# Two-layer hybrid backbone on one core: packed early loads, own tiles for the mLSTM's z gates, the second layer's output gate by a broadcast DMA

## The chip, the cores and the metric

The kernel runs on one core of a Trainium2 chip. The metric is device time in microseconds (us) of one execution; lower is better. Before the change the median of three runs is 1688.14 us (1687.44 to 1690.84).

## What is computed

Two layers act on 256 latent tokens `x` and 256 context tokens `ctx` of width 1024. The modulation of a layer comes from `c` (for the latent tokens) and `c_ctx` (for the context). One input projection feeds three branches (a bidirectional state-space scan, differential attention, a bidirectional mLSTM), whose outputs are gated, projected, merged and projected once more. Cut to what matters here:

```python
shift, scale, gate = split(silu(c) @ w_mod + b_mod, 3)           # 1024 -> 3 * 1024, per layer
h = rms_norm(x, norm_g) * (1 + scale) + shift
p = [h @ w for w in split_cols(w_in, IN_SIZES)]                  # 14 parts
y_a = ssd_branch(p[0], p[1], p[2], ...)                          # x/B/C with a conv, z, dt
y_b = diff_branch(p[3], p[4], p[5], p[6], ...)                   # q, k, v, z
y_c = mlstm_branch(p[7], ..., p[12], ...)                        # qk, v, o, z, input and forget gates
g = sigmoid(p[13])
x = x + gate * ((g0 * (y_a @ w_branch[0]) + g1 * (y_b @ w_branch[1]) + g2 * (y_c @ w_branch[2])) @ w_out)
# the same for the context with c_ctx; only the latent stream of the last layer is returned
```

## The kernel before

All numbers are fp32. A product is made of three matmuls on parts that are rounded to fp32r: a weight is split into `whi` (ACT casts, L117) and `wlo` (DVE subtracts, L83), an activation into `hh` and `hl`, and the three matmuls are whi by hh, whi by hl and wlo by hh (L146 to L148 with tokens as rows, L177 to L179 in `proj_ch` with channels as rows). Weights arrive in granules of 512 KB (128x4x256, tile `raw`, three buffers), loaded by SP (L128).

The order of the work is not written out. A scheduler sorts each engine's instructions at build time by a priority (band 0: loads and evictions, band 1: the branches' chains, band 2: projection matmuls as filling) and by its own clock; the number of buffers of a tile limits how far a piece can run ahead. SP's loads leave in this order, from one queue.

The places that the change and the prediction's steps touch:

- **Start.** `mod_pair` (L243) loads 4 granules of `w_mod` for each of two column blocks (L255), multiplies each by the vectors in `mod_mm` (L226) and ends in `mod_tail` (L235), which adds `b_mod` into `modc`. It runs twice for layer 0, 16 granules in all: pair one serves the columns k 0 to 3, pair two k 4 to 7. Tile `wm` has 8 buffers; the last three granules go to `raw` buffers. Between the granules SP issues small loads from a list `few` (L352 to L375), two per granule in pair one and three in pair two. The four x loads (L390) come after four granules. `columns(l)` (L395) transposes a layer's rows of small parameters with 12 matmuls.
- **Normalisation of layer 0** (L468 to L511): `turn` transposes the scaled rows (L493, two per k and half), ACT applies the modulation (`hf`), POOL makes `hh` (L89) and DVE `hl` (L83).
- **Narrow gate weights** (L540 to L555): six loads of 16 or 4 columns into one `raw` tile that DVE clears first (L541, L544), the split, then the matmuls of `pg`.
- **Tables**: `narrow` (L287) has the small per-layer columns `gcol`, the products `gcs`/`gsn` of the rotary table and the norm gains, and lambda.
- **Scan of the mLSTM**, `ml_core` (L1086): per direction and chunk the matmuls L1112 (`pw` by `va`), L1117 (`uq` by the state `C`) and L1133 (`kw` by `va`), with DVE between them: `nu`, `dn` (four steps), `y`, `kw`, `C`. Its gates `zz` have two buffers, shared with the other branches' (`silu2`, L719).
- **Output gate**, L1280 to L1294: a vector per token group is spread over 128 partitions by 8 matmuls with the identity (two groups of four, L1292) and halved by ACT (L1294); DVE uses `gbc` at the very end.

Of the kernel before, what the change touches and what calls it, by code (L numbers as in the profile page):

```python
# [18 lines left out]
D = 1024  # L19
# [10 lines left out]
NR = 64  # L30
ACC, PE_, PM = 3, 3, 2
# [3 lines left out]
def hybrid_backbone_kernel(ctx: ExitStack, tc: tile.TileContext, A, out, dbg=None):  # L35
# [128 lines left out]
    def proj_ch(srcs, lhs, ranges, evac, halves=False, gr=None):  # L164
# [3 lines left out]
        with band(2):  # L168
            for i in range(2):
                ps.append(pacc())  # L170
# [25 lines left out]
        for i in range(2):  # L196
            with band(0):
                evac(i, ps[i])

# [31 lines left out]
    def mod_tail(l, cbs, row):  # L231
        with band(2):
# [3 lines left out]
            for x, cb in enumerate(cbs):  # L236
                r = 16 * l + 12 + cb // 3
# [5 lines left out]
    def mod_pair(l, cbs, pool, bufs, rbufs, between=None, each=None, end=False):  # L243
        with band(2):
            ps = pacc()
            for x, cb in enumerate(cbs):
                if x and between:
                    between()
                for k0 in range(0, KT, 2):
                    if end and x and k0 >= 2:  # L250
                        wm = mk(wts, [P, 2, 512], "raw", bufs=3)
                    else:
                        wm = mk(pool, [P, 2, 512], "wm", bufs=bufs)
# [6 lines left out]
                    mod_mm(ps, x, k0, wm)  # L260
# [26 lines left out]
    def narrow(l, pool):  # L287
# [3 lines left out]
        lamt = mk(pool, [P, 4, 64], "lamt", bufs=1)  # L291
        lp = mk(pool, [P, 2, 64], "lp", bufs=1)
# [47 lines left out]
    prow = [mk(setup, [16, 1536], f"prow{l}") for l in range(depth)]  # L340
    with band(0):
# [5 lines left out]
        for l in range(depth):  # L347
            V.memset(prow[l], 0.0)
# [3 lines left out]
        few = []  # L352
        for l in range(depth):
            w_ = prow[l]

            few += [
                (w_[12:14, :], A["b_mod"][l].rearrange("(a n) -> a n", a=2)),
                (w_[8:9, 0:D], A["norm_g"][l : l + 1]),
                (w_[0:3, :], A["ssd_conv_w"][l]),
                (w_[3:4, :], A["ssd_conv_b"][l : l + 1]),  # L360
                (w_[4:7, 0:D], A["ml_conv_w"][l]),
                (w_[7:8, 0:D], A["ml_conv_b"][l : l + 1]),
                (w_[9:10, 0:D], A["ssd_norm_g"][l : l + 1]),
                (w_[10:11, 0:D], A["ml_norm_g"][l : l + 1]),
                (w_[11:12, 0:P], A["diff_subln_g"][l : l + 1]),
            ]
            if l == 0:
                few += [(selm, A["k_selm"]), (sgn, A["k_sgn"])]
                nar = narrow(0, setup)
                few += nar[0]  # L370
                few += [(rope, A["k_rope"].rearrange("a t p d -> p a t d"))]
# [4 lines left out]

# [15 lines left out]
    def columns(l):  # L392
        pc = pm()
        for k in range(12):
            T.transpose(pc[:, 16 * k : 16 * k + 16], prow[l][:, k * P : (k + 1) * P], ident[0:16, 0:16])  # L395
        pl_ = pcols[:, :, 16 * l : 16 * l + 16]
        V.tensor_copy(pl_, pc[:, 0:192].rearrange("p (k a) -> p k a", a=16))

        tsc(pl_[:, :, 0:8], pl_[:, :, 0:8], 0.5, ALU.mult)
        lam_init = 0.8 - 0.6 * math.exp(-0.3 * l)  # L400
        tsc(pl_[:, 0, 11:12], pl_[:, 0, 11:12], 0.5 * (1.0 - lam_init), ALU.mult)
# [6 lines left out]
    first_gr = granules(bc_cols(0, 0))  # L408
    first_gr = chain([next(first_gr)], first_gr)
    mods += [  # L410
        mod_pair(0, (1, 3), setup, 8, 2, None, lambda: few_loads(3), end=True),
    ]
    with band(0):
        few_loads(99)
        columns(0)
    for t in mods:
        t()
    with band(0):
        nar[1]()
# [22 lines left out]
    for l in range(depth):  # L442
# [9 lines left out]
        pr = 16 * l  # L452
        pcol = lambda k, r: pcols[:, k, pr + r : pr + r + 1]
        wcol = lambda c, n=256: w_in[:, c : c + n]
        lam_init = 0.8 - 0.6 * math.exp(-0.3 * l)

        gcol, dbc, nlam, gcs, gsn, gctx = nar[2]
# [5 lines left out]
        with band(1):  # L463
# [19 lines left out]
            def gains(kh):  # L483
                ks = slice(4 * kh, 4 * kh + 4)
                tsc(ga[:, ks, :], modc[l][:, 8 + 4 * kh : 12 + 4 * kh, :], 1.0, ALU.add)
                tt(ga[:, ks, :], ga[:, ks, :], bc(pcols[:, ks, pr + 8], 2), ALU.mult)
# [12 lines left out]
            if l == 0:  # L499
                norm(0)  # L500
                norm(1)
                for kh in range(2):
                    gains(kh)
                    for s in range(2):
                        turn(kh, s)
            else:
                for kh in range(2):
                    gains(kh)
                for s in range(2):
                    norm(s)  # L510
                    for kh in range(2):  # L511
                        turn(kh, s)
# [4 lines left out]
        if l == 0:  # L517
            with band(0):
                for l_ in range(1, depth):
                    columns(l_)  # L520
            setup.release()
# [17 lines left out]
        with band(0):  # L539
            wsm = mk(wts, [P, KT, P], "raw", bufs=3)  # L540
            V.memset(wsm, 0.0)  # L541
            pieces = ((0, O_DT, 16), (16, O_FG, 4), (32, O_DT + 16, 16), (48, O_FG + 4, 4), (80, O_IG, 4), (112, O_IG + 4, 4))
            for c, o, n in pieces:
                nc.sync.dma_start(wsm[:, :, c : c + n], w_in[:, o : o + n].rearrange("(k p) n -> p k n", p=P))  # L544
            wsh = mk(wts, [P, KT, P], "whi", F32R, bufs=3)
            wsl = mk(wts, [P, KT, P], "wlo", F32R, bufs=3)
            split(wsm, wsh, wsl)
        with band(2):
# [866 lines left out]
```

## Time and profile before

| | |
|---|---|
| median of 3 runs | 1688.14 us (1687.44 to 1690.84) |
| profiled execution | 1688.44 us, span 1686.7 us |
| mean granted TensorE clock | 0.992 |
| PE busy | 1649.9 us, 98% of the span |
| weight loads (PEld) busy | 1470.5 us, 87% |
| DVE busy | 1093.0 us, 65% |
| ACT busy | 765.4 us, 45% |
| POOL busy | 185.1 us, 11% |
| HBM | 193.29 MB read, 116 GB/s over the span |

The span is the stretch of the profile from the first to the last instruction; 1.7 us of the execution lie around it. The page cuts the span into 40 slices of 42.2 us and shows the busy share of each in tenths, and PEclk, the granted clock, in the same way. A window is a stretch that the reader chooses; it has the busy time of each engine, the granted clock, the busy share of the 16 DMA engines and their rate. In a timeline each row is one instruction or a run of equal ones, with the idle time of its engine before it and what ended that. Matmuls overlap, so the pitch of their starts, not the duration shown, is what each adds.

### The profile page before, as it was taken

The page shows a single profiled execution, that of the slowest core. Times are in us where ns is not written, and L with a number is a line of the kernel's source. Part 1 is how long each engine was busy: PE and PEld are TensorE (multiplying, and loading weights), DVE is VectorE, ACT ScalarE, POOL GpSimd, SP SyncE. Part 2 cuts the span into 40 slices and gives each one's busy share as a digit, 9 for nine tenths or more (in the row PEclk, how much of TensorE's full clock was granted, in tenths as well). Part 3 has the DMA queues.
Part 4 walks back from the last instruction along what each step waited for, and adds up shares of the span by engine and source line. Part 5 has one row for each costly group of instructions (what it writes and reads, how often), then busy time and mean ns, then how long its engine had stood idle before and what let it go on. Part 6 is the DMA issues. An engine that isn't in the chain of part 4 may idle for free. (4 is left out here: it accounts for less than half of the span.)

```text
span 1686.7 us, 28784 instructions
## 1 busy us (share of the span) xinstructions
PE 1649.9 (98%) x11288; PEld 1470.5 (87%) x11288; DVE 1093.0 (65%) x2175; ACT 765.4 (45%) x1497; POOL 185.1 (11%) x232
## 2 busy tenths in 40 slices
PE   6999999999999999999999999999999999999998
PEld 2798789999899999977777789988899999999998
DVE  4787887767864776523334355796887767775565
ACT  3467534554554543422223233556455555444453
POOL 0114331001100000000010001022122011000100
PEclk8999999999999999999999999999999999999999
DMA  8445322222223222453544442344342325336654
GB/s 273 119 134 160 88 79 79 69 71 63 78 63 101 79 85 64 128 187 93 182 136 128 161 135 59 93 127 135 107 116 76 100 76 141 110 101 176 183 168 150
DMA packets 203653, 197.00 MB, mean 117 GB/s; under 512 B 21855, under 2 KB 184033, under 8 KB 203517
## 3 DMA queue, kind: packets, MB, share of 16 engines
q1 hardware_dynamic: 203516, 195.16, 39.4%
q8 instruction: 89, 1.46, 0.3%
q14 instruction: 48, 0.39, 0.1%
HBM read 193.29 MB, written 1.84 MB: 116 GB/s over the span
## 5 line engine op out<-in xcount | busy, mean ns | idle before, releaser
L83 DVE TENSOR_TENSOR wlo<-raw,whi 128x1024 fp32r<-128x1024 f32 x274 | 347.1, 1267 | 313.8 <-ACT whi L117 312.4
L147 PE MATMUL acc<-wlo,hh 128*128 128x256 f32 x1728 | 504.4, 292 | 0.0
L146 PE MATMUL acc<-whi,hh 128*128 128x256 f32 x1728 | 502.3, 291 | 0.0
L148 PE MATMUL acc<-whi,hl 128*128 128x256 f32 x1728 | 501.5, 290 | 0.0
L117 ACT CAST whi<-raw 128x1024 fp32r<-128x1024 f32 x274 | 287.1, 1048 | 378.1 <-PE acc L178 253.0
L147 PEld LDWEIGHTS acc<-wlo,hh 128*128 128x128 f32 x1728 | 330.1, 191 | 12.5 <-issue 9.5
L148 PEld LDWEIGHTS acc<-whi,hl 128*128 128x128 f32 x1728 | 330.2, 191 | 12.2 <-issue 10.6
L146 PEld LDWEIGHTS acc<-whi,hh 128*128 128x128 f32 x1728 | 329.8, 191 | 11.0 <-issue 8.5
L177 PE MATMUL acc<-hh,whi 128*128 128x512 f32 (+1 forms) x712 | 254.1, 359 | 1.3 <-DVE cv_a L80 1.3
L178 PE MATMUL acc<-hl,whi 128*128 128x512 f32 (+1 forms) x712 | 253.7, 357 | 0.2 <-DVE hl L83 0.2
L179 PE MATMUL acc<-hh,wlo 128*128 128x512 f32 (+1 forms) x712 | 253.1, 357 | 0.0
L177 PEld LDWEIGHTS acc<-hh,whi 128*128 128x128 f32 x712 | 135.0, 191 | 28.3 <-issue 5.9
L178 PEld LDWEIGHTS acc<-hl,whi 128*128 128x128 f32 x712 | 135.4, 190 | 19.4 <-issue 2.4
L179 PEld LDWEIGHTS acc<-hh,wlo 128*128 128x128 f32 x712 | 135.3, 190 | 19.3 <-issue 1.8
L177 PE MATMUL acc<-yh,whi 128*128 128x512 f32 (+1 forms) x384 | 128.7, 338 | 0.0
L178 PE MATMUL acc<-yl,whi 128*128 128x512 f32 (+1 forms) x384 | 128.2, 336 | 0.0
L179 PE MATMUL acc<-yh,wlo 128*128 128x512 f32 (+1 forms) x384 | 128.1, 336 | 0.0
L179 PEld LDWEIGHTS acc<-yh,wlo 128*128 128x128 f32 x384 | 71.9, 188 | 8.3
L178 PEld LDWEIGHTS acc<-yl,whi 128*128 128x128 f32 x384 | 72.1, 188 | 8.0
L968 ACT ACTIVATE E<-pe,nmax 128x512 f32<-128x512 f32 (+1 forms) x96 | 58.7, 616 | 44.8 <-DVE nmax L966 44.6
L177 PEld LDWEIGHTS acc<-yh,whi 128*128 128x128 f32 x384 | 72.0, 188 | 7.3
L811 ACT ACTIVATE ex<-ex,col 128x128 f32<-128x128 f32 x192 | 60.4, 393 | 34.8 <-POOL ex L766 31.0
(302 smaller groups left out, 2429.3 us busy)
## 6 DMA issues: line engine op xcount, KB each, us to landing
raw<-in_w_in_dram SPq DMA_DIRECT2D x192, 512.0 KB
raw<-in_w_branch_dram SPq DMA_DIRECT2D x48, 512.0 KB
wm<-in_w_mod_dram SPq DMA_DIRECT2D x45, 512.0 KB
raw<-in_w_in_dram SPq DMA_DIRECT2D x48, 256.0 KB
ex<-acs_d SPq DMA_DIRECT2D x32, 256.0 KB
raw<-in_w_out_dram SPq DMA_DIRECT2D x16, 512.0 KB
ex<-acs_d SPq DMA_DIRECT2D x32, 128.0 KB
pw<-nm_d SPq DMA_DIRECT2D x8, 256.0 KB
```

The lines of the kernel that those rows point to most:

```text
L83: (eng or V).tensor_tensor(out=o, in0=a, in1=b, op=op)
L117: S.copy(hi, raw)
L146: T.matmul(o, lhsT=xh[:, k, sl], rhs=hi[:, j, :], start=(k == 0 and i == 0), stop=False)
L147: T.matmul(o, lhsT=xh[:, k, sl], rhs=lo[:, j, :], start=False, stop=False)
L148: T.matmul(o, lhsT=xl[:, k, sl], rhs=hi[:, j, :], start=False, stop=(k == KT - 1 and i == 1))
L177: T.matmul(o, lhsT=hi[:, j, cs], rhs=xh[:, k, a:b], start=(k == 0 and first), stop=False)
L178: T.matmul(o, lhsT=hi[:, j, cs], rhs=xl[:, k, a:b], start=False, stop=False)
L179: T.matmul(o, lhsT=lo[:, j, cs], rhs=xh[:, k, a:b], start=False, stop=(k == KT - 1 and final))
L811: S.activation(ex[:, c, :], ex[:, c, :], AF.Exp, bias=col[:, LDT, c, d, h : h + 1])
L968: S.activation(e_, o, AF.Exp, bias=ng[:, m : m + 1], accum_out=rs[:, m : m + 1])
```

## The change

1. **Small loads.** The rows of both layers come packed in two tiles, one DMA per parameter: `mrow_` (b_mod, norm_g) and `prow` (the rest). One small load stands behind each `w_mod` granule instead of two or three; both tiles are transposed before the projections. The loads of `narrow` and the rotary table move behind the `w_mod` loads. `wm` has 11 buffers. The matmuls of the modulation are issued for two granules at once.
2. **First projections.** The first granule of the x projection is loaded early too, and the first two projections (B/C and x) alternate by granule, the x one in the `pe` PSUM banks; `turn` goes k by k.
3. **Narrow gate weights.** Two loads (32 and 16 columns) into a tile of their own and three DVE copies (L545 of the changed kernel) instead of six loads.
4. **z gates of the mLSTM** get own tiles (`mzz`, four buffers).
5. **Output gate of the last layer.** The vector is written to DRAM (`gate_d`) and read back over 128 partitions by one DMA; DVE halves it. The 8 matmuls and 2 ACT instructions of that layer go.

The core of the diff:

```diff
-    def proj_ch(srcs, lhs, ranges, evac, halves=False, gr=None):
+    def proj_ch(srcs, lhs, ranges, evac, halves=False, gr=None, bank=None):
...
-                ps.append(pacc())
+                ps.append((bank or pacc)())
...
+                yield
...
-                    if end and x and k0 >= 2:
-                        wm = mk(wts, [P, 2, 512], "raw", bufs=3)
-                    else:
-                        wm = mk(pool, [P, 2, 512], "wm", bufs=bufs)
+                held = []
+                    wm = mk(pool, [P, 2, 512], "wm", bufs=bufs)
...
-                    mod_mm(ps, x, k0, wm)
+                    held.append((k0, wm))
+                    if len(held) == 2:
+
+                        for k_, w_ in held:
+                            mod_mm(ps, x, k_, w_)
+                        held = []
...
+        few = [
+            (mrow_[0:4, :], A["b_mod"].rearrange("l (a n) -> (l a) n", a=2)),
+            (mrow_[4:6, 0:D], A["norm_g"]),
+            (selm, A["k_selm"]),
+            (prow[0:6, :], A["ssd_conv_w"].rearrange("l k n -> (l k) n")),
...
+            (sgn, A["k_sgn"]),
+        ]
...
-    mods = [mod_pair(0, (0, 2), setup, 8, 2, load_x, lambda: few_loads(2))]
+    mods = [mod_pair(0, (0, 2), setup, 11, 2, load_x, lambda: few_loads(1))]
+
+    first_gr = [granules(bc_cols(0, 0)), granules([A["w_in"][0][:, O_X : O_X + 256]])]
+    first_gr = [chain([next(g)], g) for g in first_gr]
...
-                for k in range(4 * kh, 4 * kh + 4):
-                    pt = (pe if k % 2 else pm)()[:, 0:256]
+                for k in kh:
+                    pt = (pe if k % 2 and l else pm)()[:, 0:256]
...
-                    for s in range(2):
-                        turn(kh, s)
+                    for k in range(4 * kh, 4 * kh + 4):
+                        for s in range(2):
+                            turn((k,), s)
...
+            wnr = mk(wts, [P, KT, 48], "raw", bufs=3)
-            pieces = ((0, O_DT, 16), (16, O_FG, 4), (32, O_DT + 16, 16), (48, O_FG + 4, 4), (80, O_IG, 4), (112, O_IG + 4, 4))
-            for c, o, n in pieces:
-                nc.sync.dma_start(wsm[:, :, c : c + n], w_in[:, o : o + n].rearrange("(k p) n -> p k n", p=P))
+            for c, o, n in ((0, O_DT, 32), (32, O_IG, 16)):
+                nc.sync.dma_start(wnr[:, :, c : c + n], w_in[:, o : o + n].rearrange("(k p) n -> p k n", p=P))
...
+                V.tensor_copy(v4(wsm[:, :, h_ : h_ + 64])[:, :, :, c % 64 : c % 64 + n], v4(wnr[:, :, o : o + 2 * n]))
+            if l == 0:
...
+                for p_ in nar[0][4:] + nar[0][:4]:
+                    nc.sync.dma_start(*p_)
+                nc.sync.dma_start(rope, A["k_rope"].rearrange("a t p d -> p a t d"))
...
-            zz = mk(ev, [P, 2, 256], "zz", bufs=2)
+            zz = mk(own, [P, 2, 256], "mzz", bufs=4) if own else mk(ev, [P, 2, 256], "zz", bufs=2)
...
-        bc_proj(0)
-        x_proj(0, 0)
-        x_proj(0, 1)
+        if l == 0:
+            run(zip_longest(bc_proj(0), x_proj(0, 0)))
+        else:
+            run(bc_proj(0))
+            run(x_proj(0, 0))
+        run(x_proj(0, 1))
...
+        if last:
+            gate_d = mk(rows_d, [D], "gate_d")
+            with band(2):
+                nc.sync.dma_start(gate_d.rearrange("(k p) -> p k", p=P), modc[l][:, 16:24, 0])
...
+                if last:
+
+                    with band(0):
+                        nc.sync.dma_start(gbc[p], gate_d.partition_broadcast(P))
+                    tsc(gbc[p], gbc[p], 0.5, ALU.mult)
+                    continue
```

What this does to the order, at three places.

SP at the start, before: the first `w_mod` loads with the small loads of `few` between them.

```order
L255 DMA wm<-in_w_mod_dram 128x2x512
L375 DMA prow_98<-in_b_mod_dram 2x1536
L375 DMA prow_98<-in_norm_g_dram 1x1024
L255 DMA wm<-in_w_mod_dram 128x2x512
L375 DMA prow_98<-in_ssd_conv_w_dram 3x1536
L375 DMA prow_98<-in_ssd_conv_b_dram 1x1536
L255 DMA wm<-in_w_mod_dram 128x2x512
```

SP at the same place in the changed kernel.

```order
L260 DMA wm<-in_w_mod_dram 128x2x512
L378 DMA mrow__98<-in_b_mod_dram 4x1536
L260 DMA wm<-in_w_mod_dram 128x2x512
L378 DMA mrow__98<-in_norm_g_dram 2x1024
L260 DMA wm<-in_w_mod_dram 128x2x512
L378 DMA selm<-in_k_selm_dram 128x4
```

One small load stands between two granules instead of two; ahead of the last `w_mod` load SP issues 57 loads before and 38 in the changed kernel, among these one more granule of 512 KB.

DVE at the start, before: the last rotary products, the `hl` of pair one (eight), the clearing of the narrow weights' tile, then the modulation and the `hl` of pair two.

```order
L83 TENSOR_TENSOR gcs<-rope,gctx 128x64
L83 TENSOR_TENSOR gsn<-rope,gctx 128x64
L83 TENSOR_TENSOR hl<-hf,hh 128x256 x8
L541 MEMSET raw 128x1024
L83 TENSOR_TENSOR modc<-acc,pcols 128x8 x2
L87 TENSOR_SCALAR ga<-modc 128x8
L83 TENSOR_TENSOR ga<-ga,pcols 128x8
L83 TENSOR_TENSOR wlo<-raw,whi 128x1024
L83 TENSOR_TENSOR hl<-hf,hh 128x256 x4
```

DVE in the changed kernel: two `hl` for k 0, then these rows (`hl` two at a time; L545 are the copies of the narrow weights; the L85 row on `raw` is lambda's).

```order
L85 TENSOR_TENSOR gcs<-rope,gctx 128x64
L85 TENSOR_TENSOR gsn<-rope,gctx 128x64
L545 COPY raw<-raw 128x8x2x16
L545 COPY raw<-raw 128x8x2x4 x2
L85 TENSOR_TENSOR hl<-hf,hh 128x256
L530 MEMSET sv 64x12
L85 TENSOR_TENSOR modc<-acc,pcols 128x8 x2
L85 TENSOR_TENSOR raw<-raw 128x128
L85 TENSOR_TENSOR hl<-hf,hh 128x256
L89 TENSOR_SCALAR ga<-modc 128x8
```

The `hl` for k 2 and 3 now stand behind the rotary products and the copies of the narrow weights, and so behind the two loads that these wait for.

PE in the first head of layer 0's mLSTM scan (`ml_core(0)`), before, with the numbers that tell the tiles apart.

```order
L177 MATMUL acc_6458<-hh_294,whi_6462 128x512
L178 MATMUL acc_6458<-hl_295,whi_6462 128x512
L1112 MATMUL pm_6312<-va_5164,pw_6286 128x257
L1117 MATMUL pe_6316<-C_6310,uq_5154 128x257
L1133 MATMUL pm_6327<-va_5164,kw_6325 128x257
L179 MATMUL acc_6458<-hh_294,wlo_6463 128x512
L177 MATMUL acc_6458<-hh_294,whi_6493 128x512
L178 MATMUL acc_6458<-hl_295,whi_6493 128x512
```

PE in the same scan in the changed kernel, where L1112, L1117 and L1133 are L1128, L1133 and L1149.

```order
L149 MATMUL acc_6808<-wlo_6867,hh_266 128x256
L150 MATMUL acc_6808<-whi_6866,hl_267 128x256
L1128 MATMUL pm_6320<-va_5153,pw_6275 128x257
L1133 MATMUL pe_6324<-C_6318,uq_5143 128x257
L1149 MATMUL pm_6335<-va_5153,kw_6333 128x257
L1128 MATMUL pm_6339<-va_5153,pw_6275 128x257
L1133 MATMUL pe_6343<-C_6337,uq_5143 128x257
L1128 MATMUL pm_6362<-va_5153,pw_6352 128x257
L1149 MATMUL pm_6374<-va_5153,kw_6372 128x257
L1128 MATMUL pm_6378<-va_5153,pw_6352 128x257
L1133 MATMUL pe_6382<-C_6376,uq_5143 128x257
L1149 MATMUL pm_6393<-va_5153,kw_6391 128x257
```

Before, 9 to 22 projection matmuls stand between two steps of this scan; in the changed kernel 17 matmuls of the scan follow each other with two projection matmuls among them, and then the four transposes of the next head.

## Rows read from the trace of the kernel before

**Rows 1.** The page: busy time of the engines, and PE's busy tenths in 40 slices.

```profile
PE 1649.9 (98%) x11288; PEld 1470.5 (87%) x11288; DVE 1093.0 (65%) x2175; ACT 765.4 (45%) x1497; POOL 185.1 (11%) x232
...
PE   6999999999999999999999999999999999999998
```

**Rows 2.** Windows at the start: us, busy times, PEclk, DMA share, GB/s.

```profile
4.00:42.40 38.40, 25.95 (x112) 8.94 (x114) 18.39 (x72) 12.36 (x30) 3.92 (x8) 0.82 0.88 294
18.00:20.00 2.00, 0.06 (x1) 0.06 (x2) 1.62 (x11) 1.96 (x7) 0.00 (x0) 0.50 1.07 382
24.00:26.00 2.00, 2.00 (x7) 0.98 (x6) 1.82 (x9) 0.00 (x0) 0.00 (x0) 0.50 0.74 197
40.00:42.00 2.00, 1.05 (x4) 0.14 (x4) 0.00 (x0) 0.00 (x0) 0.00 (x0) 1.00 0.92 348
46.00:48.00 2.00, 2.00 (x8) 1.61 (x8) 0.58 (x4) 0.00 (x0) 0.00 (x0) 0.58 0.92 44
```

**Rows 3.** Timeline of SP's queue: start, us, instruction.

```profile
14.70 0.57 SPq L375 DMA_DIRECT2D sgn<-in_k_sgn_dram  x1
17.30 0.38 SPq L255 DMA_DIRECT2D wm<-in_w_mod_dram  x1
...
30.10 0.39 SPq L375 DMA_DIRECT2D rope<-in_k_rope_dram  x1
...
43.16 3.13 SPq L544 DMA_DIRECT2D raw<-in_w_in_dram  x5
```

**Rows 4.** Timeline of ACT.

```profile
14.71 0.63 ACT L475 ACTIVATE sq<-xin 128x512 f32<-128x512 f32 x1 [6.46 <-DMA xin<-in_ctx_dram]
...
49.43 1.05 ACT L117 CAST whi<-raw 128x1024 fp32r<-128x1024 f32 x1 [4.26 <-DMA raw<-in_w_in_dram]
```

**Rows 5.** Timeline of PE around the first projection.

```profile
43.48 1.05 PE L226 MATMUL acc<-raw,cst 128*32 128x512 f32 x4 [0.23 <-DMA raw<-in_w_mod_dram]
...
46.14 0.61 PE L177 MATMUL acc<-hh,whi 128*128 128x512 f32 x1
...
49.86 0.40 PE L177 MATMUL acc<-hh,whi 128*128 128x512 f32 x1
...
53.06 0.38 PE L493 MATMUL pm<-ident,xin 128*128 128x128 f32 x2
53.28 0.27 PE L493 MATMUL pe<-ident,xin 128*128 128x128 f32 x1
...
57.24 0.91 PE L395 MATMUL pm<-ident,prow 16*128 16x16 f32 x12
```

**Rows 6.** Timeline of DVE: the rotary products and `hl`.

```profile
33.49 0.23 DVE L83 TENSOR_TENSOR gcs<-rope,gctx 128x64 f32<-128x64 f32 x1 [0.32 <-DMA rope<-in_k_rope_dram]
...
35.21 3.77 DVE L83 TENSOR_TENSOR hl<-hf,hh 128x256 fp32r<-128x256 f32 x8
```

**Rows 7.** Critical chain near the output gate: start, us, what.

```profile
1620.91 0.89 PE pm L1292 x8
```

**Rows 8.** Timeline of PE: one step of the mLSTM scan.

```profile
561.15 0.60 PE L1117 MATMUL pe<-C,uq 128*128 128x257 f32 x2
561.59 0.60 PE L1133 MATMUL pm<-va,kw 128*128 128x257 f32 x2
```

**Rows 9.** Timeline of DVE: the same step.

```profile
562.51 0.48 DVE L80 SCALAR_TENSOR_TENSOR nu<-pe,mlc,nu 128x257 f32<-128x257 f32 x1
562.90 0.47 DVE L80 SCALAR_TENSOR_TENSOR C<-C,mlc,pm 128x257 f32<-128x257 f32 x1
...
564.15 0.14 DVE L87 TENSOR_SCALAR dn<-nu 128x1 f32<-128x1 f32 x1
564.33 0.16 DVE L83 TENSOR_TENSOR dn<-dn,nu 128x1 f32<-128x1 f32 x1
```

**Rows 10.** Windows of layer 0's state-space region, columns as in rows 2.

```profile
100.00:260.00 160.00, 151.33 (x989) 130.92 (x988) 128.86 (x202) 87.44 (x216) 53.34 (x52) 0.99 0.40 116
...
180.00:190.00 10.00, 8.07 (x49) 6.66 (x48) 8.81 (x12) 5.11 (x10) 4.67 (x3) 1.00 0.19 53
```

More of the change, by code (lines that the diff above doesn't have):

```diff
@@ L2 @@
 from contextlib import ExitStack, contextmanager
-from itertools import chain
+from itertools import chain, zip_longest
 import concourse.bass as bass
@@ L198, in proj_ch, with run @@
                 evac(i, ps[i])
+    def run(steps):
+        for _ in steps:
+            pass
     def rsqrt(src, n, scale, eps, pp=P, pool_=True):
@@ L241, in mod_tail, with mod_pair @@
                 )
-    def mod_pair(l, cbs, pool, bufs, rbufs, between=None, each=None, end=False):
+    def mod_pair(l, cbs, pool, bufs, rbufs, between=None, each=None):
         with band(2):
@@ L339, in hybrid_backbone_kernel @@
     xin0 = [mk(nrm0, [P, D], "xin", bufs=4) for _ in range(NT)]
-    prow = [mk(setup, [16, 1536], f"prow{l}") for l in range(depth)]
+    mrow_ = mk(setup, [6, 1536], "mrow_")
+    prow = mk(setup, [22, 1536], "prow")
     with band(0):
@@ L346, in hybrid_backbone_kernel @@
         V.memset(cst, 0.0)
-        for l in range(depth):
-            V.memset(prow[l], 0.0)
+        V.memset(mrow_, 0.0)
+        V.memset(prow, 0.0)
         V.memset(ones, 1.0)
         V.memset(mhalf, -0.5)
[L352 to L371, printed above, removed]
+        few = [
[3 more added lines that the diff above has]
+            (prow[0:6, :], A["ssd_conv_w"].rearrange("l k n -> (l k) n")),
+            (prow[6:8, :], A["ssd_conv_b"]),
+            (prow[8:14, 0:D], A["ml_conv_w"].rearrange("l k n -> (l k) n")),
+            (prow[14:16, 0:D], A["ml_conv_b"]),
+            (prow[16:18, 0:D], A["ssd_norm_g"]),
+            (prow[18:20, 0:D], A["ml_norm_g"]),
+            (prow[20:22, 0:P], A["diff_subln_g"]),
+            (sgn, A["k_sgn"]),
+        ]
         def few_loads(n):
@@ L390, in load_x, with columns @@
                 nc.sync.dma_start(xin0[t], (A["ctx"] if t < 2 else A["x"])[0][(t % 2) * P : (t % 2 + 1) * P, :])
[L392 removed]
+    def columns(rows, c0):
+        n = rows.shape[0]
         pc = pm()
         for k in range(12):
[L395 to L401, printed above, removed]
+            T.transpose(pc[:, n * k : n * k + n], rows[:, k * P : (k + 1) * P], ident[0:n, 0:n])
+        V.tensor_copy(pcols[:, :, c0 : c0 + n], pc[:, 0 : 12 * n].rearrange("p (k a) -> p k a", a=n))
     def bc_cols(l, g):
         return [A["w_in"][l][:, c : c + P] for c in (O_B + P * g, O_C + P * g)]
[L406 to L409 removed]
+    mods = [mod_pair(0, (0, 2), setup, 11, 2, load_x, lambda: few_loads(1))]
+    first_gr = [granules(bc_cols(0, 0)), granules([A["w_in"][0][:, O_X : O_X + 256]])]
+    first_gr = [chain([next(g)], g) for g in first_gr]
     mods += [
[L411 removed]
+        mod_pair(0, (1, 3), setup, 11, 2, None, lambda: few_loads(1)),
     ]
     with band(0):
+        columns(mrow_, 22)
         few_loads(99)
[L415 removed]
+        columns(prow, 0)
+        tsc(pcols[:, :, 0:16], pcols[:, :, 0:16], 0.5, ALU.mult)
+        for l in range(depth):
+            lam_init = 0.8 - 0.6 * math.exp(-0.3 * l)
+            tsc(pcols[:, 0, 20 + l : 21 + l], pcols[:, 0, 20 + l : 21 + l], 0.5 * (1.0 - lam_init), ALU.mult)
     for t in mods:
         t()
[L418 to L419 removed]
     pending = []
@@ L510, in hybrid_backbone_kernel @@
                     norm(s)
-                    for kh in range(2):
-                        turn(kh, s)
+                    turn(range(KT), s)
         hT = (hh, hl)
```

70 lines of the change are left out of this document (37 added, 33 removed).

## The prediction

> **What bounds the kernel now.** I read the page first: PE is busy 1649.9 us of a span of 1686.7 us, and of the 40 slices only the first is at 6 tenths and the last at 8 [rows 1]. PE is the bound nearly everywhere; an edit pays only if it takes PE work away or fills one of the few places where PE waits. Then I looked for these places in windows and timelines. The largest is the start: the first projection matmul runs at 46.14, after the last `w_mod` load has landed at 43.48 [rows 5]. The second is layer 0's state-space region, where PE is busy 151.3 of 160 us while DVE is at 81%, and at 88% in the window shown in which PE waits 1.9 of 10 us [rows 10]. The end is short. The start is therefore read as a stretch that loads bound, the middle as PE with DVE as second.
>
> **The loads at the start.** From 4.0 to 42.4 us the DMAs move 294 GB/s on the mean; with the x loads in flight it is 382, with `w_mod` granules alone 348, in the thin windows down to 197 [rows 2]. Why it gets thin is seen on SP: the load of `sgn`, the 24th, is issued at 14.70, when ACT's wait for the first x load, the 16th, ends (14.71), and the next granule only at 17.30 [rows 3, 4]. So eight loads are open at once, and a load of a few bytes takes one of the eight places as a granule does. The changed kernel puts one small load behind a granule instead of two or three and issues 38 loads instead of 57 ahead of the last granule.
>
> The bytes: 294 GB/s times 38.4 us are 11.29 MB. The second first-projection granule adds 0.52 MB; the tables moved behind (lambda 131 KB, rotary 131 KB, gains 66 KB) take 0.33 away: 11.48 MB. At 348 GB/s that is 33.0 us, at 382 it is 30.1, at the old mean of 294 it is 39.0. The last byte is at 42.4 before, 1.1 us ahead of the landing. I take 344 GB/s, nearest to the window with granules alone, since most of the bytes are granules: 4.0 + 33.4 + 1.1 = 38.5 for the landing, **5.0 us earlier**. Ends: 35.2 (382 throughout, 8.3 earlier) and 44.1 (294 throughout, 0.6 later).
>
> The Trainium skill, DMA: Bandwidth & Descriptors, Specifications, gives about 358 GB/s as the limit from HBM for one core. By it the landing would be at 4.0 + 32.1 + 1.1 = 37.2, and the sum 1.3 us lower; the 382 GB/s of the window with x loads is above that limit, so the trace does not bear it out here.
>
> **Behind the last load.** Call its landing L. The path L to first projection was 2.66 us before [rows 5]; two granules at once and the transposes add little, so the projection starts at about L + 2.9. It has `hl` of k 0 and k 1 ready: 12 matmuls, the first nine at a granted clock near half, 0.58 in the window [rows 2] (46.14 to 49.86, 0.41 each), the others 0.23 each (49.86 to 53.06 are 14) [rows 5], then four transposes, 0.5: `hl` of k 2 is wanted at L + 7.8. DVE makes it only after the rotary products and the copies of the narrow weights. The rotary table is issued about L + 0.8; before it took from 30.10 to about 33.4, when DVE's wait for it ends [rows 3, 6], so it lands near L + 4.0; eight products take 1.72 us (33.49 to 35.21), three copies about 0.9, taken like two `hl`, two `hl` 0.94 (0.47 each) [rows 6]: L + 7.6, in time by a hair. The narrow weights come in two loads instead of six, with a third of the pieces (2 times 1024 against 6 times 1024, one per row and k). Before they took from 43.16 to 49.43, 6.3 us, with the queues 92% busy at 44 GB/s in between [rows 2 to 4]: such small pieces are paid by the piece. With a third of the pieces they land near L + 5, just ahead of the copies. Wait on PE: between 0 and 2.9 (if they take as long as before); I take **+1.0**.
>
> The Trainium skill, same page and section, says that a transfer under 512 bytes makes the engine read, modify and write, so it does not reach line rate. The pieces grow from 64 and 16 bytes to 128 and 64, still below. If that makes the time go with the bytes, which stay the same 196 KB, the loads would land 2.9 us later and the sum would be about 2 us higher; if it goes with the pieces, as I take it, nothing changes. The trace of before has no second size to decide it.
>
> PE work around the start: 20 transposes of x follow the start of the projections instead of 6, 14 more at 0.11 (53.06 to 53.28 for two), **+1.5**; the 12 of the second layer's parameters, 0.91, go ahead of it, **-0.9** [rows 5]. The start in all: -5.0 + 1.0 + 1.5 - 0.9 = **-3.4** (ends -7.7 and +4.1).
>
> **Output gate.** The two groups of 8 matmuls stand on the critical chain with 0.89 us each [rows 7] (the second, as long, at 1623.21): **-1.8**. What comes in is off the chain: a vector written some 100 us earlier, a read of 512 KB that is issued long before DVE uses `gbc`, and a DVE scaling of 128x1024. DVE is at 65% [rows 1], so that hides; if it did not, it would cost about 1.2 us, the time of a 128x1024 DVE instruction.
>
> **The mLSTM's z tiles and the order they bring.** Tiles of their own let the z gates of the mLSTM run before the consumers of the other branches. That takes no wait away that I can find: PE hardly waits there. But the scheduler's order changes. In `ml_core(0)` of layer 0, 17 matmuls of the scan now follow each other with two projection matmuls between, where before 9 to 22 covered each step. PE's own time for them is 17 times 0.43 (561.15 to 561.59) [rows 8] and 0.8 for the four transposes and the two, 8.1 us. DVE has 5 `nu`, 4 `C` and 4 `y` at 0.39, and 22 small ones (`dn`, `kw`) at about 0.19 (starts 562.51, 562.90; 564.15, 564.33) [rows 9]: 5.1 + 4.2 = 9.3 us. If DVE alone is the bound: 9.3 - 8.1 = +1.2. If each `C` waits for its matmul and each matmul for its `C`, five times 0.6 us [rows 8] add to DVE: +4.2. After such a wait PE runs at half clock for some us, as at 46.14 to 49.86, where nine matmuls cost 0.18 more each, 1.7 [rows 5]. I take **+3.5**, the middle of the two plus half of the clock; ends +1 and +7 (every hand-over alone, both directions in turn).
>
> **State-space region.** Its chains now run later against the projections, with query, key and value projections ahead. PE's 8.7 us of waiting [rows 10] can shrink or be met elsewhere; I cannot read it from the order, since it is DVE's backlog that decides. Taken at **0**, ends -6 and +3. Second layer: its order is the same but for the gate: 0.
>
> **Sum.** -3.4 - 1.8 + 3.5 + 0 = -1.7 against the profiled execution, 1688.44: 1686.7. The median is 0.3 lower, so **1686.4**. Two kernels of this length can be told apart by about 0.2%, 3.4 us, so this is "no change", on the faster side.
>
> **The rivals.**
>
> 1. *The state-space region opens up (faster).* With 20 us more of projections ahead of the first scan, DVE works off its splits and evictions before the scan needs it, and the scan's steps meet a free DVE. For it: DVE is at 8.8 of 10 us where PE waits most, against 81% over the whole stretch, so it has slack elsewhere. Against: the total of DVE's work is the same, and what is done earlier must have been idle there. Price: 6 of the 8.7 us: -7.7, **1680.4**. It decides if DVE's busy share in the region stays under 0.8.
> 2. *The start does not move (slower).* The place is the load stretch: if the 294 GB/s are what the channels give for this mix and not the small loads' doing, the landing stays at 44.1 (+0.6), the waits behind the rotary table and the narrow weights come in full (+1.0 to 2.9), and the transposes remain (+0.6): about +2.2 for the start, with +3.5 from the bare scan and -1.8: +3.9, **1692.0**. For it: the windows are at 1.0 busy share with x loads, so there is no slack to use there; against: 348 GB/s and 0.92 near the end of the same stretch, and 197 at 0.74 where small loads stand in the queue. It decides if the last granule lands after 42.
> 3. *The bare scan is dearer.* If every hand-over in `ml_core(0)` is alone and the clock falls through it: +7 instead of +3.5, **1689.9**. It decides if PE's waits on L1128 to L1149 there sum to over 5 us.
>
> **How the numbers follow.** Chances: forecast 0.42, rival 1 0.25, rival 2 0.20, rival 3 0.13. Faster by over 0.2% means under 1684.8: most of rival 1 (0.21) and the forecast's lower part, with the load ends (0.14): 0.35. Slower by over 0.2%, above 1691.5: rival 2 in its larger half (0.13), rival 3 with a weaker start (0.05) and a tail of the forecast (0.02): 0.20. The rest, 0.45, is the same. The range takes in rival 1 and rival 2: 1680.0 to 1692.5. The forecast's own range is 1683 to 1690.
>
> **What would show it.** In the changed kernel's profile the last `w_mod` matmul should wait for its load until 37 to 40, the first projection start at 40 to 43, and PE wait 0 to 3 us on `hl` within the first 8 us after. L1292's counterpart should be gone from the second layer. `ml_core(0)` should show PE waits of 2 to 5 us on DVE in about 15 us, with half clock near it. Wrong would be: a landing after 42; waits of the region 100 to 280 that differ from 9 us by over 4; any new wait in the second layer.

## The result and the profile after

The changed kernel takes 1704.06 us (median of 4 runs, 1702.17 to 1705.47) against 1688.72 us before: ratio 1.0095, 95% interval 1.0079 to 1.0111. It is slower by 15 us where 1.7 us less were forecast. The profiled execution has a span of 1700.4 us, 13.7 more than before; it is the one that the following goes by. (Run times of this program scatter by about 2 us from one execution to the next; one run of before_gate_rows below, 4356.08 us, lies far outside and stands in no ratio.)

The page of the changed kernel: span, busy times, PE's slices and its granted clock.

```profile
span 1700.4 us, 28736 instructions
...
PE 1650.5 (97%) x11272; PEld 1468.8 (86%) x11272; DVE 1085.2 (64%) x2181; ACT 765.3 (45%) x1495; POOL 186.6 (11%) x232
...
PE   6999999999999899999999998999999999999998
...
PEclk7999999999999999999999999999999999999999
```

PE is as busy as before [rows 1] (+0.6 us), so the 13.7 us are waiting. Two slices in the middle have dropped to 8. Windows of 40 us place them; first the kernel before, where PE was never idle there, then the changed one. The columns are those of [rows 2].

```profile
520.00:560.00 40.00, 40.00 (x284) 37.20 (x283) 23.96 (x64) 20.69 (x46) 2.54 (x4) 1.00 0.31 93
560.00:600.00 40.00, 40.00 (x298) 38.53 (x296) 28.27 (x85) 17.44 (x41) 2.52 (x4) 1.00 0.34 96
1000.00:1040.00 40.00, 40.00 (x340) 40.00 (x339) 20.74 (x29) 10.58 (x17) 0.90 (x2) 1.00 0.49 123
```

```profile
520.00:560.00 40.00, 36.13 (x252) 31.82 (x252) 19.91 (x40) 16.16 (x36) 0.00 (x0) 1.00 0.26 75
560.00:600.00 40.00, 34.85 (x242) 31.20 (x242) 28.60 (x96) 23.03 (x61) 5.26 (x7) 1.00 0.23 67
1000.00:1040.00 40.00, 34.07 (x259) 33.08 (x258) 22.23 (x30) 13.75 (x19) 0.00 (x0) 0.91 0.49 124
```

PE waits 3.9 and 5.2 us at the end of the attention and in the first mLSTM scan, 9.0 together, and 5.9 us at the boundary of the layers. The waits of 530 to 610 us in the changed kernel (place, waited for, us in total, times, longest):

```profile
PE pm L1128 <- ACT nu L1130: 1.8, 1, 1.8
PE acc L179 <- DVE cv_a L82: 1.7, 1, 1.7
PE acc L148 <- DVE cv_a L82: 1.5, 1, 1.5
PE pm L1114 <- ACT rt L1003: 1.2, 1, 1.2
```

The first is the scan's; the next two are filling projections that wait at the attention's end for an accumulator that DVE is still reading; in the fourth the scan's first matmuls wait for the attention's last norm on ACT. The wait at the boundary was not in any rival. PE's and SP's timelines of the changed kernel show it, then ACT's.

```profile
1021.00 0.28 PE L150 MATMUL acc<-whi,yc 128*128 128x256 f32 x1
1027.21 0.58 PE L148 MATMUL acc<-whi,yb 128*128 128x256 f32 x1 [5.93 <-DVE otmp L85]
...
1031.18 0.28 PE L148 MATMUL acc<-whi,yb 128*128 128x256 f32 x1
```

```profile
1005.56 0.37 SPq L1242 DMA_DIRECT2D gate_d<-modc  x1
1006.69 2.10 SPq L1368 DMA_DIRECT2D raw<-in_w_out_dram  x2
```

```profile
1019.39 1.05 ACT L119 CAST yh<-raw 128x1024 fp32r<-128x1024 f32 x1 [11.46 <-DMA raw<-in_w_out_dram]
```

The write of the gate vector is issued at 1005.56, two `w_out` loads right behind it; ACT then waits 11.46 us for a `w_out` load, until 1019.39. In the 10 us between, the DMAs move next to nothing:

```profile
1006.00:1008.00 2.00, 2.00 (x19) 2.00 (x18) 2.00 (x3) 1.91 (x4) 0.00 (x0) 1.00 0.27 10
1008.00:1010.00 2.00, 2.00 (x20) 2.00 (x19) 1.00 (x2) 0.00 (x0) 0.00 (x0) 1.00 0.03 8
...
1014.00:1016.00 2.00, 2.00 (x19) 2.00 (x19) 0.00 (x0) 0.00 (x0) 0.00 (x0) 1.00 0.47 28
...
1018.00:1020.00 2.00, 2.00 (x19) 2.00 (x19) 0.00 (x0) 0.61 (x1) 0.00 (x0) 1.00 0.98 350
```

The DMA packets of two stretches, 1006.4 to 1007.2 and then 1007.2 to 1016, tell the write and the loads apart:

```profile
DMA packets 1040, 0.00 MB, mean 5 GB/s; under 512 B 1040, under 2 KB 1040, under 8 KB 1040
```

```profile
DMA packets 232, 0.24 MB, mean 27 GB/s; under 512 B 0, under 2 KB 232, under 8 KB 232
```

The write's 1024 pieces of 4 bytes (and 16 more packets as small) are through within 0.8 us. It is the loads behind them that crawl, 232 packets in 8.8 us.

After the wait 19 matmuls from 1027.21 to 1031.18 run at the lower clock (0.51 granted, 1.2 GHz): 3.97 us, where they take 2.24 at the pitch of 0.118 of the rows ahead (1020.88 to 1021.00): 1.7 more. So the boundary costs 5.9 + 1.7 = 7.6.

At the start the sum is near the forecast by luck, for the road is another. The rows answer to [rows 5].

```profile
27.92 1.92 PE L233 MATMUL acc<-wm,cst 128*32 128x512 f32 x4 [3.23 <-DMA wm<-in_w_mod_dram]
...
35.44 3.08 PE L233 MATMUL acc<-wm,cst 128*32 128x512 f32 x10
...
41.52 1.07 PE L233 MATMUL acc<-wm,cst 128*32 128x512 f32 x8
...
44.21 0.48 PE L179 MATMUL acc<-hh,whi 128*128 128x512 f32 x1
```

The loads are through at about 36 (383 GB/s at 32 to 34, 30 at 36 to 38 in windows of 2 us), but from 27.92 to 44.21 PE works almost without a wait (0.12 us), up to 38 at half clock (0.50 to 0.54 in the windows from 28), on the modulation's matmuls and the transposes between. The first projection is 1.9 us earlier, not 5, and then runs at full clock at once, where before nine matmuls took 1.7 us too much [rows 5].

Where the 13.7 us are, by three places that both traces have:

| stretch | before | after | difference |
|---|---|---|---|
| to the first projection | 46.14 | 44.21 | -1.9 |
| from there to the first transpose of the second layer | 994.4 | 1012.0 | +17.7 |
| from there to the end | 646.2 | 644.2 | -2.0 |

The middle row holds 9.0 (attention's end and scan), 7.6 (boundary), 0.8 (the region from 80 to 280 us: waits of 9.55 against 8.79), +0.6 transposes and -1.7 of clock: 16.3 of 17.7; the rest is spread. The last row can't be read as the gate's 1.8: the same stretch takes 644.53 in no_gate below, which has the gate's matmuls.

### The profile page after: what moved, and what is told of

The parts are those of the page before. It is cut to its first block, busy times and chain, and to the rows that moved or that the text cites. A ratio compares the mean times of both kernels' runs of the same rounds, so it can differ in the third digit from the quotient of the medians.

```text
span 1700.4 us, 28736 instructions
## 1 busy us (share of the span) xinstructions
PE 1650.5 (97%) x11272; PEld 1468.8 (86%) x11272; DVE 1085.2 (64%) x2181; ACT 765.3 (45%) x1495; POOL 186.6 (11%) x232
## 5 line engine op out<-in xcount | busy, mean ns | idle before, releaser
L85 DVE TENSOR_TENSOR wlo<-raw,whi 128x1024 fp32r<-128x1024 f32 x274 | 343.5, 1254 | 295.9 <-ACT whi L119 294.7
L179 PE MATMUL acc<-hh,whi 128*128 128x512 f32 (+1 forms) x696 | 246.6, 358 | 3.1 <-DVE cv_a L82 3.1
L180 PE MATMUL acc<-hl,whi 128*128 128x512 f32 (+1 forms) x696 | 247.2, 356 | 0.2 <-DVE hl L85 0.2
L181 PE MATMUL acc<-hh,wlo 128*128 128x512 f32 (+1 forms) x696 | 247.2, 357 | 0.0
L181 PEld LDWEIGHTS acc<-hh,wlo 128*128 128x128 f32 x696 | 131.7, 190 | 19.5 <-issue 2.5
```

The source lines that it names most:

```text
L85: (eng or V).tensor_tensor(out=o, in0=a, in1=b, op=op)
L179: T.matmul(o, lhsT=hi[:, j, cs], rhs=xh[:, k, a:b], start=(k == 0 and first), stop=False)
L180: T.matmul(o, lhsT=hi[:, j, cs], rhs=xl[:, k, a:b], start=False, stop=False)
L181: T.matmul(o, lhsT=lo[:, j, cs], rhs=xh[:, k, a:b], start=False, stop=(k == KT - 1 and final))
```

## The experiments

Waits are PE's. Ratios are to the kernel before, on the same chip.

**no_gate**: the changed kernel with the gate by matmuls again.

```diff
-            gate_d = mk(rows_d, [D], "gate_d")
-                nc.sync.dma_start(gate_d.rearrange("(k p) -> p k", p=P), modc[l][:, 16:24, 0])
...
-                        nc.sync.dma_start(gbc[p], gate_d.partition_broadcast(P))
-                    tsc(gbc[p], gbc[p], 0.5, ALU.mult)
-                    continue
```

> The changed kernel with the last layer's gate made by the eight matmuls and two ACT instructions again; the rest as changed. Theory W (the write of the gate vector, 128x8 pieces of 4 bytes, holds up the w_out loads that stand behind it in SP's queue): PE's wait of 5.9 us at the layer boundary and the about 1.9 us at half clock behind it go, the gate's 1.8 us of matmuls come back: 6.0 us less than the changed kernel, about 1698. Rival O (that wait comes from the other order at the boundary, with the copies of the narrow weights in DVE's queue and the later x loads): the wait stays at about 6 us and the time is 1.8 us above the changed kernel, about 1706.

Measured: 1696.79, ratio 1.0049 (1.0034 to 1.0064); no wait at the boundary, the others as in the changed kernel (3.9 and 5.3). **before_gate** is its mirror: the kernel before with these lines put in.

> The kernel before with only the gate by write and broadcast load. Theory W: the same 6.0 us as a loss, about 1694 to 1695, with a wait of some 6 us at the layer boundary. Rival O: no wait there, 1.8 us faster, about 1687.

Measured: 1697.70, ratio 1.0055 (1.0040 to 1.0070), with a wait of 6.2 us at the boundary, on `otmp` as in the changed kernel. That is 10.7 over the kernel before where W put 6 to 8: between the first projection and the second layer its profile has 7.9 more, the wait and the half clock behind it, and the rest lies outside that stretch. The loss at the boundary goes and comes with the gate's edit, of which only the write stands there (the read is issued some 520 us later): W holds, O falls.

**gate_act_queue** and **before_gate_rows** ask what it is in the write. The second edit is shown against before_gate.

```diff
-                nc.sync.dma_start(gate_d.rearrange("(k p) -> p k", p=P), modc[l][:, 16:24, 0])
+                nc.scalar.dma_start(gate_d.rearrange("(k p) -> p k", p=P), modc[l][:, 16:24, 0])
```

> The changed kernel with the write of the gate vector issued by ACT instead of SP, everything else in the same order. Theory Q (the loads wait because they stand in the same queue behind the write): the wait of about 6 us at the layer boundary goes; with the gate's matmuls gone as well the time is 1.8 us under no_gate, 8 us over the kernel before. Theory C (the DMA engines themselves are held by 1024 pieces of 4 bytes, whatever queue they come from): the wait stays at 4 us or more and the time stays 15 us over the kernel before.

```diff
-                nc.sync.dma_start(gate_d.rearrange("(k p) -> p k", p=P), modc[l][:, 16:24, 0])
+                pt8 = pm()
+                T.transpose(pt8[0:KT, 0:P], modc[l][:, 16:24, 0], ident)
+                gate_r = mk(small, [KT, P], "gate_r")
+                V.tensor_copy(gate_r, pt8[0:KT, 0:P])
+                nc.sync.dma_start(gate_d.rearrange("(k p) -> k p", p=P), gate_r)
```

> The kernel before with the gate by write and broadcast load, but the vector is first turned by one matmul into 8 rows of 128, so that the write has 8 pieces of 512 bytes. By Q and by C alike the small pieces are what takes the time: no wait at the boundary, and the gate's matmuls (1.8 us) less one transpose (0.1): 1.5 to 1.8 us faster than the kernel before, ratio about 0.999. Rival R (any write ahead of the w_out loads holds them): a wait of 5 us or more stays.

Measured: from ACT's queue 1704.10, ratio 1.0102 (1.0088 to 1.0116), as slow as the change. ACT's timeline there:

```profile
1007.91 0.39 ACTq L1242 DMA_DIRECT2D gate_d<-modc  x1
...
1021.30 1.05 ACT L119 CAST yh<-raw 128x1024 fp32r<-128x1024 f32 x1 [11.03 <-DMA raw<-in_w_out_dram]
```

The loads stand in SP's queue and wait 11.03 us all the same: it is not SP's queue (Q falls), but something that both queues share (C). Whether that is the engines themselves is not shown: the pieces pass them in 0.8 us.

With 8 pieces of 512 bytes there is no wait at the boundary: 1686.53, ratio 1.0001 (0.9992 to 1.0010). But this run changes two things. The transpose is filling work, and the order puts it, and with it the write, over 500 us later. SP's queue in before_gate_rows, where before_gate has its write at 998.85:

```profile
1520.10 0.30 SPq L1230 DMA_DIRECT2D gate_d<-gate_r  x1
1523.18 0.35 SPq L1300 DMA_DIRECT2D gbc<-gate_d  x1
1523.63 0.39 SPq L128 DMA_DIRECT2D raw<-in_w_in_dram  x1
```

So no write stands ahead of the `w_out` loads of the first layer any more, and R is not tested there. At the new place the rows hold nothing for long: SP waits 2.7 us for the write before it issues the read, and the two loads issued 3.1 and 3.5 us behind the write move soon after their issue (199 and 355 GB/s):

```profile
1524.00:1526.00 2.00, 2.00 (x19) 2.00 (x18) 1.46 (x2) 1.06 (x2) 0.00 (x0) 1.00 0.87 199
1526.00:1528.00 2.00, 2.00 (x19) 2.00 (x19) 0.72 (x2) 1.52 (x3) 0.00 (x0) 1.00 1.01 355
```

That speaks against R and for the small pieces, but no run has a write by rows at the boundary, or 4-byte pieces at the later place. The 1.8 us of the gate are there when one looks where they must be, in the last stretch. From the first `yh` of the last branch on ACT to PE's last matmul, before and then in before_gate_rows:

```profile
1612.42 0.46 ACT L92 ACTIVATE yh<-pm,pcols 128x256 fp32r<-128x256 f32 x1
...
1681.87 0.28 PE L148 MATMUL acc<-yh,yc 128*128 128x256 f32 x1
```

```profile
1615.94 0.47 ACT L92 ACTIVATE yh<-pm,pcols 128x256 fp32r<-128x256 f32 x1
...
1683.59 0.28 PE L148 MATMUL acc<-yh,yc 128*128 128x256 f32 x1
```

69.45 and 67.65 us: 1.80 less (67.66 in the changed kernel, 1627.77 to 1695.43). From run to run the rest scatters by as much, and the ratio cannot tell it: the 1.5 to 1.8 us expected in the total were not seen.

**no_z** and **no_gate_no_z**: the shared z tiles again.

```diff
-                zzs[p] = silu2(ps, mp_)
+                zzs[p] = silu2(ps)
```

> The changed kernel with the mLSTM's z gates back in the shared tiles (two buffers); the rest as changed. Theory Z (the own z tiles let the filling projections run early, so the end of the attention and the first mLSTM scan stand bare): PE's waits between 520 and 600 us fall from 9.0 to 3 or less, since only seven scan matmuls in a row are left bare instead of seventeen: 5 to 6 us less than the changed kernel, about 1698. Rival S (the new order of the start alone empties the filling): the waits stay at 7 or more, about 1702 to 1704.

> The changed kernel with both taken back: only the packed loads, the interleaved first projections and the two narrow loads are left. If the parts add up (W and Z): 6 and 5.5 us less than the changed kernel, 1692 to 1693, which is 4 above the kernel before, so that the start would cost something by itself through the order it brings. By S: about 1698.

Measured: 1707.79, ratio 1.0120 (1.0103 to 1.0137), and 1703.89, ratio 1.0092 (1.0077 to 1.0107). Z falls, and S only has the cause right: the waits from 520 to 600 us do not stay, they rise to 13.2 and 12.8, and taking the own tiles out makes it slower, by 4 us (from the changed kernel) and by 7 (from no_gate). The bare run is shorter, as read from the order, but another wait stands in its place (waits of no_gate_no_z from 520 to 640 us):

```profile
PE pm L1128 <- DVE pw L85: 6.9, 1, 6.9
PE acc L179 <- DVE cv_a L82: 1.7, 1, 1.7
PE acc L148 <- DVE cv_a L82: 1.5, 1, 1.5
```

`pw` is late because DVE does the attention's last products first; in the changed kernel it does `pw` (570.88) ahead of them (571.89). DVE in no_gate_no_z:

```profile
569.42 2.94 DVE L82 SCALAR_TENSOR_TENSOR yb<-yb,riB,zz 128x128 f32<-128x128 f32 x8
572.45 0.94 DVE L85 TENSOR_TENSOR pw<-pw,scT 128x512 f32<-128x512 f32 x1
```

The own tiles are the remedy for an order in which the z projection wants its tiles while the attention still holds them (pack_only below shows that wait); the loss of filling is there with the start's edits alone. **z_only** is the kernel before with the own tiles.

> The kernel before with own tiles for the mLSTM's z gates alone. By the order every scan step keeps 16 or more filling matmuls around it. Theory F (only missing filling costs): no waits of PE between 520 and 640 us, time within 2 us of before. Rival Z2 (the own tiles bring the z gates forward and take the filling by themselves): waits of 3 us or more there.

Measured: 1686.78, ratio 0.9997 (0.9988 to 1.0006), no wait from 520 to 640 us. In the order of before they cost nothing and give nothing.

**no_gate_va3** tests the cause of the waits in the scan.

```diff
-            va = mk(mlin, [P, NT, 257], "va", bufs=2)
+            va = mk(mlin, [P, NT, 257], "va", bufs=3)
```

> no_gate with a third buffer for the mLSTM's value tile va, which lets the next head's projections run ahead: by the order, 6 scan matmuls of the first head stand bare instead of 17. Theory F (the scan is dear because its filling projections have nowhere to write): PE's waits between 560 and 600 us fall from 5.3 to 2 or less, and the time by 3 to 4 us, to about 6 over the kernel before. Rival E (the waits are DVE's lateness from the attention, whatever stands between): they stay within 1 us of 5.3.

Measured: 1693.55, ratio 1.0039 (1.0026 to 1.0053), 3.2 us under no_gate. The window of 560 to 600 us, in no_gate and then here:

```profile
560.00:600.00 40.00, 34.67 (x244) 31.07 (x243) 27.42 (x94) 21.41 (x55) 4.55 (x6) 1.00 0.23 67
```

```profile
560.00:600.00 40.00, 38.90 (x291) 36.85 (x289) 26.57 (x85) 20.12 (x50) 3.99 (x5) 1.00 0.33 93
```

5.3 us of waits become 1.1 (and 0.7 in the next window): the scan was dear for want of filling, and a buffer gives it back (F). The 3.9 us ahead of it, at the attention's end, stay.

**no_interleave**: no_gate with the first two projections one after the other.

```diff
-    first_gr = [granules(bc_cols(0, 0)), granules([A["w_in"][0][:, O_X : O_X + 256]])]
+    first_gr = [granules(bc_cols(0, 0))]
...
-            run(zip_longest(bc_proj(0), x_proj(0, 0)))
+        run(bc_proj(0))
+        run(x_proj(0, 0))
```

> no_gate with the first projections one after the other again and one early granule instead of two; packed loads, own z tiles and the two narrow loads stay. Theory I (the alternation is what moves the chains against the filling): the waits between 520 and 600 us fall from 9.2 to about 4 (by the order nine scan matmuls in a row are left bare), the time to 4 to 5 over the kernel before. Rival P (the packed start alone does it): the waits stay at 7 or more.

Measured: 1690.07, ratio 1.0021 (1.0003 to 1.0039); waits from 520 to 600 us 3.5 instead of 9.2. The alternation, with its early granule, is what moves the chains most (I).

**pack_only** and **pack_own_z**: the packed start without the alternation, the old `turn`, six narrow loads, no gate DMA; with shared and with own z tiles (the no_interleave edit, the old lines of `turn` and of the narrow loads, and the z line above).

> The kernel before with the start's loads alone changed: packed rows, the tables behind the last granule, 11 buffers, the modulation's matmuls two granules at once. No alternation, six narrow loads, shared z tiles, the gate by matmuls. Theory H (the loads end several us earlier, but PE, at half clock with the modulation's matmuls, takes over as the bound): last w_mod byte near 36 as in the changed kernel, first projection only 1 to 3 us earlier than 46.1; waits of 2 to 3 us in the first mLSTM scan (by the order four scan matmuls stand bare at its end): within 2 us of the kernel before. Rival L (the start is bound by loads): first projection 5 us earlier and the time 3 us or more under before.

> pack_only with own tiles for the mLSTM's z gates. In pack_only PE waits 5.5 us for a z gate (zz) whose two shared tiles the attention still holds. Theory Y (the packed start moves the attention's end against the mLSTM's z gates, and own tiles are what takes that wait away): the wait on zz goes; by the order nine scan matmuls in a row are left bare instead of four, some 2 to 3 us of waits there as in no_interleave: 3 us less than pack_only, 4 to 5 us over the kernel before. Rival X (the wait only changes its name): the waits between 520 and 640 us stay at 6 us or more.

Measured: 1694.69, ratio 1.0050 (1.0034 to 1.0065), and 1691.56, ratio 1.0031 (1.0019 to 1.0042). In pack_only the first projection does start early, at 41.44, right behind the last load:

```profile
38.59 1.05 PE L233 MATMUL acc<-wm,cst 128*32 128x512 f32 x4 [0.96 <-DMA wm<-in_w_mod_dram]
...
41.44 0.78 PE L179 MATMUL acc<-hh,whi 128*128 128x512 f32 x1
```

Yet it is slower than before: 4.7 us are won at the start, and 6.5 lost to waits between 520 and 600 us, of which

```profile
PE acc L148 <- DVE zz L82: 5.5, 1, 5.5
```

stands for the shared z tiles. H and L both expected a gain or a draw, and both miss. With own tiles that line is gone, the waits there are 3.4 instead of 6.5 and the time is 3.1 less (Y).

**repair_all**: the changed kernel with the gate by rows and a third `va`. **best**: that, with the no_interleave edit. **best_old_turn**: best with the old `turn` and six narrow loads.

> The changed kernel whole, with two repairs: the gate vector is written as 8 rows of 512 bytes, and va has a third buffer. If the two causes are additive and the whole loss but the rest of the alternation's: 7.8 less for the boundary and its half clock, 3.2 less for the scan: 4 to 5 us over the kernel before.

> The same two repairs, and the first projections one after the other: packed loads, own z tiles, two narrow loads, gate by rows. By the order no scan step is bare. From no_interleave (2.9 over before, with 3.5 us of waits in the scan) less the waits and the gate's 1.7: 2 to 3 us under the kernel before, ratio 0.998 to 0.999. If it is not under before, the packed start costs something that the waits don't show.

> The version best with the old order of the transposes and the six narrow loads, that is pack_only with own z tiles, a third va buffer and the gate by rows. If the first projection of pack_only (41.4, against 45.6 in best) is kept and no scan step is bare: 3 us under best and the kernel before, ratio 0.998. If the earlier start is lost behind it (waits and half clock between 40 and 280 us that grow as it starts earlier): within 0.1% of before.

Measured: 1691.97, ratio 1.0028 (1.0016 to 1.0041), 4.9 us over the kernel before, where 4 to 5 were expected: the two repairs give back some 10 to 11 of 15 us. In this run and the next two, too, the write by rows is issued late (1524.2, 1518.9 and 1514.3). 1686.70, ratio 0.9996 (0.9986 to 1.0006), and 1686.87, ratio 0.9997 (0.9988 to 1.0006): with no scan step bare the loss is gone, but the gain does not show. In best PE kept the full clock at the start and caught up with the loads, and the last one is issued later (34.73, against 30.87 in the changed kernel), so that PE waits for it:

```profile
38.46 1.42 PE L233 MATMUL acc<-wm,cst 128*32 128x512 f32 x4 [1.80 <-DMA wm<-in_w_mod_dram]
...
45.63 0.77 PE L179 MATMUL acc<-hh,whi 128*128 128x512 f32 x1
```

Behind it the projection began only at 45.63, since narrow gate matmuls (a wait of 1.2 on `wlo`) and half clock lie between. No version was faster than the kernel before by more than its measurement can tell.

## Why the prediction was wrong

- **The output gate** is the step that failed worst. The saving was right: 1.8 forecast, 1.80 measured in the last stretch. But what came in was put at nothing, because it was off the chain, "a vector written some 100 us earlier". The write is issued 519 us ahead of its read (1005.56 and 1525.0), has 1024 pieces of 4 bytes and stands, in SP's order, between the `w_out` loads of the first layer. I thought of its own reader, not of the loads that it delays: 7.6 us. The narrow weights were paid by the piece in the same text; by that reading of [rows 2 to 4] (6144 pieces in 6.3 us) 1024 pieces would have been put at about 1 us. That is near the 0.8 us in which they pass, and a tenth of the time for which the loads behind them crawl. So the size would have been missed all the same, but not the place. Why the loads crawl is open.
- The Trainium skill, DMA: Bandwidth & Descriptors, Specifications, on transfers under 512 bytes (read, modify, write), I weighed against the narrow weights: if it made the time go with the bytes, it would have cost 2 us. There the trace bears out the count of the pieces: at the boundary before, six loads issued from 1010.36, behind two of 256 KB, kept ACT waiting until 1018.03, 7.7 us (6.3 at the start [rows 3, 4]), while in the changed kernel the two loads, with the same bytes, are issued at 1025.57 and copied by DVE at 1028.81 without a wait, 3.2 us or less. The rule also covers the gate's write, with 4 bytes a piece; the runs agree that such a write is dear. Whether reading, modifying and writing is the reason no run shows: the pieces pass in 0.8 us, and what follows them is slow.
- **The bare scan** was seen, and its price of +3.5 was near the 3.6 us of waits inside it (2.7 on its own matmuls, 0.9 on the filling that is left). The 0.8 in it for half clock did not come: the granted clock is 1.00 from 520 to 600. What the step missed is that the want of filling begins earlier: 3.9 us at the attention's end, 3.2 of them filling projections that wait for their accumulators, and 1.2 where the scan's first matmuls wait for the attention's last norm. With 0.4 on a z gate it is 9.0 in all, above the upper end of +7.
- **The reason given for it was wrong.** I put the new order down to the z tiles. They are worth 4 to 7 us in the new order and nothing in the old one (no_z, no_gate_no_z, z_only); the alternation of the first projections is worth 5.7 us of those waits, the packed start some of the rest. The forecast said of the z tiles that they take no wait away: in this order they do.
- **The start**: -3.4 forecast; measured -1.9, -1.7 for the half clock that is gone and +0.6 for transposes, -3.0. The -1.7 was in no term, so that the agreement is luck. Read closely, the last byte before came at 43.0 and not at 42.4 (65 GB/s between), so the landing was 0.5 behind it and the forecast's own sum gives 38.0 for it, not 38.5. In the changed kernel the loads were faster than the 344 GB/s taken, 360 on the mean from 4 to 36, and nearly through at 36; their landing does not decide, as PE at half clock is later. The landings that can be seen, 38.46 in best and 38.59 in pack_only, fit the forecast by luck: there the last load is issued only at 34.73 and 34.31, and the DMAs move 47 and 59 GB/s from 34 to 36. L + 2.9 holds in pack_only (41.44). The wait on `hl` of k 2, put at +1.0, did not occur.
- **The state-space region**: 0 forecast, +0.8 measured. Second layer: only the gate, as said.
- **The rivals**: 1 did not happen; 2 did not (the loads did move); 3 was the nearest in size, with 9.0 for +7, but not by its own sign: PE's waits on L1128 to L1149 are 2.7, not over 5; and it was too small without the boundary. With the measured sizes the sum is -3.0 - 1.8 + 9.0 + 7.6 + 0.8 = +12.6 of the 13.7 measured. What spreads the last us is open.

Not settled: why exactly the alternation empties the filling at the attention's end, 500 us later. The experiments show that it does, and that a buffer cures the scan; which of the scheduler's choices in between carries it was not tried. Nor was it tried whether the write with its small pieces would cost nothing at a place where no load is waited for.

## What to carry to other kernels

Ask of a transfer how many pieces it has, not only how many bytes, and which loads are on the way when it goes: with a 4 KB write of 4-byte pieces ahead, from either queue, ACT waited 11 us for `w_out` loads. One transpose that makes rows of it, and by which the write also came 500 us later, took the wait away; which of the two did it was not separated. After a repair, look where the instruction now stands. Where a scheduler sorts the work, an edit at the start can strip the filling from a serial chain hundreds of us later, so follow every chain through the new order, and look at the stretch ahead of a bare chain as well. An extra buffer for the chain's inputs is a cheap test of such a diagnosis.

## What was not expected of the hardware

- The write of 1024 pieces of 4 bytes passes in 0.8 us, and for 9 us after it DMA rates are 8 to 44 GB/s at busy shares of 0.03 to 0.47; loads of another queue wait as long (11.03 us against 11.46).
- The granted clock at the start differs between executions of kernels with the same start: 0.50 from 20 to 22 us in the changed kernel, 1.00 in no_gate and repair_all. So a term for the clock that is read from one execution each, like the -1.7 us, can come out otherwise in the next.
